# Gate, v and the ssm branch of a hybrid block in pairs of 512 columns: a quad of weights a step, 22 of 64 quads with seven block products, and memory pools opened part by part

## The chip, the cores and the metric

One core of a Trainium2 chip runs the whole program. Its engines run side by side, each its own list of instructions in order: TensorE (PE; its weight loads are shown apart as PEld), VectorE (DVE), ScalarE (ACT), GpSimd (POOL) and SyncE (SP), which here issues nearly all loads. Engines wait for each other and for DMAs through semaphores. The metric is the device time in microseconds (us) of one execution, the median of several runs. Line numbers such as L306 are lines of the kernel before; those of the changed kernel are named as such.

## The reference, cut to what matters

One layer of a hybrid block over 256 positions and 2048 channels, in f32: dilated window attention with 16 heads, beside a state space branch (SSD scan), both gated and merged.

```
hn = rms_norm(x, norm_w)
q, k, v, z_a, z_s, xbc, dt, g_a, g_s = split(hn @ w_in)
o_a = dilated_attention(q, k, v) * silu(z_a)
y = rms_norm(ssd_scan(silu(conv(xbc)), dt) * silu(z_s), ssm_norm_w)
merged = sigmoid(g_a) * (o_a @ w_attn_branch) + sigmoid(g_s) * (y @ w_ssm_branch)
out = rms_norm(x + merged @ w_out, final_norm_w)
```

Three of the products are touched: `hn @ v columns` (2048 by 2048), `y @ w_ssm_branch` (4096 by 2048) and `hn @ g_a columns` (2048 by 2048).

## The kernel before

**Products in f32 from two halves.** A weight tile w is rounded by ScalarE into a high part h (L201), and VectorE takes the low part l = w - h (L203). The left-hand side is split the same way. A block product is three matmuls into the same bank of PSUM: high by high, high by low, low by high.

**Weights.** The host lays all weights out in units of 128x1024 (512 KB), in the order in which they are used (`PLAN`); a unit is fetched, split and used once. They pass through one pool, `stream`, with four buffers each for w, h and l, which is open through the whole kernel. So SyncE may fetch four units ahead of TensorE at any place, across the end of a stage too. Rounding and low part are emitted at a raised priority (`L_AHEAD`), ahead of other work on their engines.

**Order of the stages.** Up to 590 us the ssm inputs xs and zs are projected, convolved and scanned, group by group, with the ssm gate gs. The scan writes y, split, into the tiles yT (L521: each by ScalarE L208 and VectorE L212). Then, with `gemm_b` (L283), one block of 512 columns at a time in two banks, one for each half of the rows:

- v (L572), 590 to 678 us: columns of `w_in`, left-hand side XT; ScalarE copies the banks into vt (L575).
- the ssm branch (L588), 678 to 854 us: left-hand side yT. Ahead of it four small matmuls (tot_y, L581) give the sum of squares of y, `rsqrt_rows` (L316) turns it into a factor by row, with one operation on GpSimd (L320), and two ScalarE operations apply it to the gate th_s (L587). Each finished bank is multiplied into th_s (L592).
- attention by heads (L635), 854 to 1160 us: q, k and za of each head, then scores, softmax and the mix with v, which stand some ticks behind (`after`, `tick`).
- the attention gate ga (L650), 1160 to 1250 us, into th_a.
- the attention branch (L671), from 1250 us, then the output product (L683) and the final norm.

`gemm_b` holds the inner loop, whose three matmuls are L306, L307 and L308:

```
for kt, i in steps:
    h, l = (a[:, kt % UB, :] for a in hl[kt // UB])
    pe.matmul(accs[i], xh, h, start=(kt == 0), stop=False)
    pe.matmul(accs[i], xh, l, start=False, stop=False)
    pe.matmul(accs[i], xl, h, start=False, stop=(kt == n_kt - 1))
```

The order of the instructions on each engine comes from a scheduler that simulates the program with its priorities. Constants (masks, distances, identity, ones) lie in one tile, cst, loaded once (L368).

Of the kernel before, what the change touches and what calls it, by code (L numbers as in the profile page):

```python
# [1 line left out]

# [1 line left out]

# [44 lines left out]
def weight_plan():  # L49
    plan = []  # L50

    def cols(tag, src, off, n_kt):
        plan.append((tag, "a", src, off, n_kt, P))

    def rows(tag, src, off, n_kt):
        plan.append((tag, "b", src, off, n_kt, 512))

    plan.append((("first", 0), "m", "w_in", (OFF_B, OFF_C, OFF_X, OFF_ZS), KT, 512))
    plan.append((("dt", 0), "a", "w_in", OFF_DT, KT, SH))
    for g in range(GROUPS):  # L60
# [9 lines left out]
    for c in range(4):  # L70
        rows(("v", c), "w_in", OFF_V + c * 512, KT)
    for c in range(4):
        rows(("ssm", c), "w_ssm_branch", c * 512, 2 * KT)
# [4 lines left out]
    for c in range(4):  # L78
        rows(("ga", c), "w_in", OFF_GA + c * 512, KT)
# [66 lines left out]


@with_exitstack
def hybrid_block(ctx: ExitStack, tc: tile.TileContext, wall, xt, x, pk_d, cst_d, fw_d, out):
# [19 lines left out]
    cst = cpool.tile([P, N_CST], F32, name="cst", tag="cst")  # L169
    dist_c, count_c = cst[:, 0:384], cst[:, 384:768]  # L170
    mask3 = cst[:, 768:1152]
    ident = cst[:, 1152:1280]
    ones = cst[:, 1280:1408]
    sel = cst[:, 1408:1536]
# [136 lines left out]
    def gates(tag, th, src, scales=(0.5, 0.5)):  # L311
        accs = gemm_b(tag, lambda kt: src[:, kt, :])
        for i in range(2):
            ac.activation(th[:, i, tag[1] * 512 : tag[1] * 512 + 512], accs[i], AF.Tanh, scale=scales[i])

    def rsqrt_rows(sums, n, name):  # L316
        var = lead.tile([P, 2], F32, name=f"var_{name}", tag="var", bufs=1)
        ve.tensor_scalar(var, sums, 1.0 / n, EPS, ALU.mult, ALU.add)
        r = lead.tile([P, 2], F32, name=f"r_{name}", tag="rr", bufs=1)
        gp.tensor_tensor(r, var, half, ALU.pow)  # L320
        hr = cpool.tile([P, 2], F32, name=f"hr_{name}", tag="hr", bufs=2)
        ve.tensor_scalar(hr, r, 0.5, None, ALU.mult)
        return r, hr

# [31 lines left out]
    def load_on(u):  # L356
        if u < 6:
            load(u + 4)
        if u < 3:
            nc.sync.dma_start(xr[:, 2 * u + 10 : 2 * u + 12, :], xt[:, 2 * u + 10 : 2 * u + 12, :])  # L360
        if u == 3:
            nc.sync.dma_start(pk[:, KT:], pk_d[:, KT:])
        if u == 6:

            for late in (th_s[:, 0, 0:1], cst[:, 0:1]):
                gp.tensor_copy(late, yT[0][:, 13, 0:1].bitcast(F32))
            nc.sync.dma_start(th_s, x.rearrange("(i p) d -> p i d", p=P))
# [19 lines left out]
    with tc.tile_pool(name="ssm", bufs=2) as sp:  # L387
        def dt_chain(acc):
            used = []

# [176 lines left out]
        gates(("gs", 3), th_s, XT)  # L567
        tick(final=True)

    with tc.tile_pool(name="att", bufs=2) as ap:  # L570
        vt = ap.tile([P, 2, D], F32, name="vt", tag="vt", bufs=1)
        for c in range(4):  # L572
            accs = gemm_b(("v", c), lambda kt: XT[:, kt, :])
            for i in range(2):
                ac.activation(vt[:, i, c * 512 : (c + 1) * 512], accs[i], AF.Copy)  # L575


        tot = bank("m1", 2, "tot_y")
        for i in range(2):
            for n in range(2):  # L580
                pe.matmul(  # L581
                    tot[:, 2 * i : 2 * i + 2], ssq[:, n, i * P : (i + 1) * P], ones[:, 0:2],
                    start=(n == 0), stop=(n == 1),
                )
        _, hr = rsqrt_rows(tot[:, 0:4:2], INNER, "y")
        for i in range(2):
            ac.activation(th_s[:, i], th_s[:, i], AF.Identity, scale=hr[:, i : i + 1], bias=hr[:, i : i + 1])  # L587
        for c in range(4):  # L588
            accs = gemm_b(("ssm", c), lambda kt: yT[kt // 16][:, kt % 16, :], n_kt=2 * KT)
            for i in range(2):  # L590
                g = th_s[:, i, c * 512 : (c + 1) * 512]
                ve.tensor_tensor(g, g, accs[i], ALU.mult)  # L592


        oaT = big.tile([P, 16, 2 * S], F32R, name="oaT", tag="yo0")

# [49 lines left out]
            evac(project(("za", h)), zh, f"za{h}", scale=0.5)  # L646
            half_silu(zh, za, f"za{h}")

        th_a = big.tile([P, 2, D], F32, name="th_a", tag="yo1")
        for c in range(4):  # L650
            gates(("ga", c), th_a, XT)
        tick(final=True)

    with tc.tile_pool(name="fin", bufs=2) as fp:
# [86 lines left out]
```

## Time and profile before

| what | before |
|---|---|
| median of 3 runs | 1421.44 us (1421.27 to 1422.06) |
| span of the profiled execution | 1419.2 us |
| TensorE busy | 1406.4 us (99%) |
| VectorE busy | 920.5 us (65%) |
| ScalarE busy | 760.2 us (54%) |
| bytes moved by DMA | 272.31 MB, mean 192 GB/s |

The span runs from the first to the last recorded instruction. The page gives no other time for the profiled execution, so the span stands beside the median. Shares of busy time are means over the whole span. Rows of groups give, behind the tiles, their shapes and a count: busy time in sum, mean ns of one instruction, and the engine's idle time just before them with what ended it. Rows of a timeline give the start, the duration and the instruction. Rows of windows give a stretch, the busy time and count on each engine, the clock granted to TensorE (1.00 is full), the DMAs' busy share and their rate.

### The profile page before, as it was taken

The page shows a single profiled execution, that of the slowest core. Times are in us where ns is not written, and L with a number is a line of the kernel's source. Part 1 is how long each engine was busy: PE and PEld are TensorE (multiplying, and loading weights), DVE is VectorE, ACT ScalarE, POOL GpSimd, SP SyncE. Part 2 cuts the span into 40 slices and gives each one's busy share as a digit, 9 for nine tenths or more (in the row PEclk, how much of TensorE's full clock was granted, in tenths as well). Part 3 has the DMA queues.
Part 4 walks back from the last instruction along what each step waited for, and adds up shares of the span by engine and source line. Part 5 has one row for each costly group of instructions (what it writes and reads, how often), then busy time and mean ns, then how long its engine had stood idle before and what let it go on. Part 6 is the DMA issues. An engine that isn't in the chain of part 4 may idle for free.

```text
span 1419.2 us, 19641 instructions
## 1 busy us (share of the span) xinstructions
PE 1406.4 (99%) x7404; PEld 1194.6 (84%) x7404; DVE 920.5 (65%) x1336; ACT 760.2 (54%) x1170; POOL 9.6 (1%) x63
## 2 busy tenths in 40 slices
PE   9999999999999999999999999999999999999997
PEld 7788888888888888888888888888888888888886
DVE  5978888877787888644444446666666654455654
ACT  6656766747575757444533334454544544444443
POOL 0000000000000000000000000000000000000000
PEclk9999999999999999999999999999999999999999
DMA  8566656566656665566566666555555557666663
GB/s 338 183 205 222 197 174 208 169 208 201 189 169 208 194 186 183 167 195 195 187 193 194 192 193 191 176 169 175 170 173 176 168 177 280 193 192 180 191 192 121
DMA packets 77759, 272.31 MB, mean 192 GB/s; under 512 B 8736, under 2 KB 9184, under 8 KB 77024
## 3 DMA queue, kind: packets, MB, share of 16 engines
q1 hardware_dynamic: 77088, 270.01, 60.5%
q8 instruction: 58, 0.95, 0.3%
q10 hardware_dynamic: 576, 1.05, 0.2%
q14 instruction: 37, 0.30, 0.1%
HBM read 268.86 MB, written 2.16 MB: 191 GB/s over the span
## 4 chain that ended last, share of the span: by engine, by line
PE 97%; DVE 1%; issue 0%; DMA 0%; ACT 0%; SPq 0%; POOL 0%; POOLq 0%; DVEq 0%; ACTq 0%
PE ps_xs L240 8%; PE ps_zs L240 8%; PE ps_xs L243 4%; PE ps_q L240 4%; PE ps_zs L243 4%; PE ps_za L240 4%; PE ps_k L240 4%; PE ps_ssm L306 4%; PE ps_ssm L308 4%; PE ps_ssm L307 4%; PE ps_za L243 2%; PE ps_k L243 2%; PE ps_q L243 2%; PE ps_v L306 2%; PE ps_attn L306 2%; PE ps_attn L308 2%
## 5 line engine op out<-in xcount | busy, mean ns | idle before, releaser
L203 DVE TENSOR_TENSOR l<-w,h 128x1024 fp32r<-128x1024 f32 (+1 forms) x481 | 583.1, 1215 | 430.6 <-ACT h L201 428.2
L201 ACT ACTIVATE h<-w 128x1024 fp32r<-128x1024 f32 (+1 forms) x481 | 505.3, 1052 | 573.2 <-PE ps_ssm L308 101.1
L240 PE MATMUL ps_xs<-XT,h 128*128 128x512 f32 x496 | 176.3, 397 | 0.0
L240 PE MATMUL ps_zs<-XT,h 128*128 128x512 f32 x496 | 175.8, 397 | 0.0
L243 PE MATMUL ps_xs<-XT,l 128*128 128x256 f32 x496 | 139.6, 281 | 0.0
L243 PE MATMUL ps_zs<-XT,l 128*128 128x256 f32 x496 | 139.0, 280 | 0.0
L240 PEld LDWEIGHTS ps_zs<-XT,h 128*128 128x128 f32 x496 | 93.1, 188 | 22.6
L240 PEld LDWEIGHTS ps_xs<-XT,h 128*128 128x128 f32 x496 | 93.2, 188 | 22.2
L308 PE MATMUL ps_ssm<-h,yT 128*128 128x512 f32 x256 | 99.6, 389 | 0.0
L307 PE MATMUL ps_ssm<-l,yT 128*128 128x512 f32 x256 | 99.6, 389 | 0.0
L306 PE MATMUL ps_ssm<-h,yT 128*128 128x512 f32 x256 | 99.4, 389 | 0.0
L243 PEld LDWEIGHTS ps_xs<-XT,l 128*128 128x128 f32 x496 | 93.6, 189 | 0.1
L243 PEld LDWEIGHTS ps_zs<-XT,l 128*128 128x128 f32 x496 | 93.6, 189 | 0.0
L240 PE MATMUL ps_q<-XT,h 128*128 128x512 f32 x256 | 90.4, 392 | 0.0
L240 PE MATMUL ps_za<-XT,h 128*128 128x512 f32 x256 | 89.6, 392 | 0.0
L240 PE MATMUL ps_k<-XT,h 128*128 128x512 f32 x256 | 89.6, 391 | 0.0
L243 PE MATMUL ps_q<-XT,l 128*128 128x256 f32 x256 | 74.5, 291 | 0.0
L243 PE MATMUL ps_k<-XT,l 128*128 128x256 f32 x256 | 71.7, 280 | 0.0
L243 PE MATMUL ps_za<-XT,l 128*128 128x256 f32 x256 | 71.7, 280 | 0.0
L240 PEld LDWEIGHTS ps_q<-XT,h 128*128 128x128 f32 x256 | 47.9, 187 | 10.6
L240 PEld LDWEIGHTS ps_k<-XT,h 128*128 128x128 f32 x256 | 47.9, 187 | 10.6
L240 PEld LDWEIGHTS ps_za<-XT,h 128*128 128x128 f32 x256 | 47.9, 187 | 10.6
(235 smaller groups left out, 2553.5 us busy)
## 6 DMA issues: line engine op xcount, KB each, us to landing
w<-in_wall SPq DMA_DIRECT2D x480, 512.0 KB, 3.6
acb<-acum_d SPq DMA_DIRECT2D x32, 256.0 KB, 3.2
th_s<-in_x SPq DMA_DIRECT2D x1, 2048.0 KB, 9.6
fin<-in_x SPq DMA_DIRECT2D x1, 2048.0 KB, 8.1
early<-in_xt SPq DMA_DIRECT2D x7, 256.0 KB, 7.0
fw<-in_fw SPq DMA_DIRECT2D x1, 1024.0 KB, 10.1
out<-fin SPq DMA_DIRECT2D x4, 256.0 KB, 2.9
out<-fin ACTq DMA_DIRECT2D x4, 256.0 KB, 3.2
```

Source lines behind the costliest of these rows:

```text
L201: ac.activation(h[:, a:b], w[:, a:b], AF.Copy)
L203: eng.tensor_tensor(l[:, a:b], w[:, a:b], h[:, a:b].bitcast(F32), ALU.subtract)
L240: pe.matmul(acc[:width], h[:, kk, :], m, start=(kt == 0), stop=False)
L243: pe.matmul(acc[:width, S:], l[:, kk, :], m[:, :S], start=False, stop=(kt == n_kt - 1))
L306: pe.matmul(accs[i], xh, h, start=(kt == 0), stop=False)
L307: pe.matmul(accs[i], xh, l, start=False, stop=False)
L308: pe.matmul(accs[i], xl, h, start=False, stop=(kt == n_kt - 1))
```

## The change

**Order.** The ssm branch now follows the scan at once, then the attention gate ga, then v, then attention by heads. v is written into one tile together with th_a (`yo1`).

**Quads.** The three products no longer use `gemm_b` but `quads`: two passes of 1024 columns. A step is a quad of weights, two blocks of 128 rows by two of 512 columns, laid out by the host for one load of 128x2048 (1 MB, `wq`, `lay_quads`). With two halves of the rows, a quad is a product of a 2x2 by a 2x2 matrix of blocks. All eight banks of PSUM are accumulators. Most quads take eight block products of three matmuls. 22 of the 64 (5 of 16 in each pass of the ssm branch, 3 of 8 in each of ga and v) take seven, in the manner of Strassen and Winograd: VectorE forms sums of the weight blocks (t13, t24), and sums of the left-hand blocks once for each product (`left`), all split into high and low parts; further sums on VectorE carry the products' accumulators into the four results. The ssm branch has three buffers for q and six for h and l each; ga and v have four and eight.

**Pools.** The weights' pools are opened by `stage` or for each part: one for the scan, `mid` for the ssm branch, `mid2` for ga and v, one for attention, one for the rest. A part's tiles lie where those of the part before lay. Of the constants, the distances and counts are loaded as masks when the attention part opens, and the identity a second time (ident2).

The diff, cut to its core:

```
+QPLAN = (("ssm", "w_ssm_branch", 0, 2 * KT), ("ga", "w_in", OFF_GA, KT), ("v", "w_in", OFF_V, KT))
...
-    stream = ctx.enter_context(tc.tile_pool(name="stream", bufs=4))
-    ev = ctx.enter_context(tc.tile_pool(name="ev", bufs=2))
...
+    @contextmanager
+    def stage(name):
+        nonlocal stream, ev
+        with (
+            tc.tile_pool(name=f"st_{name}", bufs=4) as stream,
+            tc.tile_pool(name=f"ev_{name}", bufs=2) as ev,
+            tc.tile_pool(name=name, bufs=2) as pool,
+        ):
+            yield pool
...
+    def left(tmp, src, n, h3, l3, h4, l4):
...
+            ve.tensor_tensor(x, v[:, js, :, :S].bitcast(F32), v[:, js, :, S:].bitcast(F32), ALU.add)
...
+            ve.tensor_tensor(s1, a22, a21, ALU.subtract)
+            ve.scalar_tensor_tensor(s2, s1, -1.0, a11, ALU.mult, ALU.subtract)
+            ve.tensor_tensor(s3, a11, a21, ALU.subtract)
+            ve.tensor_tensor(s4, a12, s2, ALU.add)
+            for r, h, l in ((raw[:, :, :3], h3[:, js], l3[:, js]), (s4, h4[:, js], l4[:, js])):
+                ac.activation(h, r, AF.Copy)
+                ve.tensor_tensor(l, r, h.bitcast(F32), ALU.subtract)
+
+    def quad(pool, deep, n, seven):
+        q = pool.tile([P, 2048], F32, name=f"q{n}", tag="q", bufs=deep[0])
+        nc.sync.dma_start(q, wq[n])
...
+            ac.activation(h[:, cut:], src[:, cut:], AF.Copy)
+            ve.tensor_tensor(l[:, cut:], src[:, cut:], h[:, cut:].bitcast(F32), ALU.subtract)
...
+        with tc.high_priority(L_AHEAD):
+            halves(q[:, :1024], ("12", "11"), 512 if seven else 0)
+            if seven:
...
+                ve.tensor_tensor(t24[:, :512], t13[:, :512], q[:, 1024:1536], ALU.add)
+                ve.tensor_tensor(t24[:, 512:], t24[:, :512], q[:, 1536:], ALU.add)
+            halves(q[:, 1024:], ("22", "21"))
+            if seven:
+                halves(t13, (5, 7))
+                halves(t24, (6, 4))
...
+            if u in lefts:
+                s1, s2, s3, s4 = lefts[u]
+                z = u == last
+                product(1, block(k0, 0), w["11"], z)
+                product(2, block(k1, 0), w["21"], end)
+                product(3, s4, w["22"], end)
+                product(7, s3, w[7], z)
+                product(5, s1, w[5], z)
+                product(6, s2, w[6], z)
+                product(4, block(k1, 1), w[4], end)
+            else:
+                for b, i, c in ((2, 0, "1"), (3, 0, "2"), (4, 1, "1"), (8, 1, "2")):
+                    product(b, block(k0, i), w["1" + c])
+                    product(b, block(k1, i), w["2" + c], end)
+            if u == last:
+                (p1, u4), (u3, u5) = sums
+                ac.activation(p1, accs[1], AF.Copy)
+                ve.tensor_tensor(u4, accs[6], p1, ALU.add)
+                ve.tensor_tensor(u3, accs[7], u4, ALU.add)
+                ve.tensor_tensor(u4, accs[5], u4, ALU.add)
+                ve.tensor_tensor(u5, accs[5], u3, ALU.add)
...
+    with tc.tile_pool(name="mid", bufs=2) as mid:
...
+        def gated(i, c, a, b, op):
+            g = th_s[:, i, c * 512 : (c + 1) * 512]
+            ve.tensor_tensor(b, a, b, op)
+            ve.tensor_tensor(g, g, b, ALU.mult)
...
+            quads(mid, (3, 6), "ssm", cc, lambda kt: yT[kt // 16][:, kt % 16, :], 2 * KT, order, lefts, sums, gated)
...
+    with tc.tile_pool(name="mid2", bufs=2) as mid:
...
+                quads(mid, (4, 8), tag, cc, lambda kt: XT[:, kt, :], KT, order, some, sums, finish)
+
+    with stage("att") as ap:
+        masks = ap.tile([P, 768], F32, name="masks", tag="masks", bufs=1)
+        nc.sync.dma_start(masks, cst_d[:, :768])
```

Three places in the built order follow. A row gives the line of its own kernel, the operation, the tile written and those read (numbers behind names tell copies of a tile apart), the shape, and in brackets the semaphores that the instruction waits for: an engine's name, or DMAHW for a DMA's landing.

SyncE at the end of the scan, where the next product's weights are fetched. Before, w193 and those behind it are the units of v:

```order
L187 DMA w191_6057<-in_wall 128x1024 [waits DMAHW2_49,DVE_49]
L187 DMA w192_6075<-in_wall 128x1024 [waits DMAHW3_49,DVE_49]
L187 DMA w193_6140<-in_wall 128x1024 [waits DMAHW4_49,DVE_49]
L187 DMA w194_6158<-in_wall 128x1024 [waits DMAHW5_49,DVE_49]
L187 DMA w195_6176<-in_wall 128x1024 [waits DMAHW6_49,DVE_49]
```

And in the changed kernel, where q0, q2, q4 and q1 are the first quads of the ssm branch:

```order
L205 DMA w191_6062<-in_wall 128x1024 [waits DMAHW3_49,DVE_49]
L205 DMA w192_6080<-in_wall 128x1024 [waits DMAHW4_49,DVE_49]
L615 DMA q0_6193<-in_wq 128x2048 [waits DMAHW5_49,DMAHW0_49,DMAHW6_49,DVE_49,DMAHW7_49,PE_49,Pool_49]
L615 DMA q2_6231<-in_wq 128x2048
L615 DMA q4_6265<-in_wq 128x2048
L615 DMA q1_6299<-in_wq 128x2048 [waits DMAHW1_49,DVE_49]
```

The first load behind the scan now waits for TensorE and GpSimd too, beside VectorE, and is one of three that leave together.

ScalarE at the same place, from the last square of y (xs15) on. Before, the copies that follow are those of v's weights:

```order
L514 ACTIVATE xs15_5739<-y1_15_6123 128x512 [waits DVE_49]
L208 ACTIVATE yT1_4244<-y1_15_6123,pk_75 128x256 x2
L201 ACTIVATE h197_6214<-w197_6212 128x1024 [waits DMAHW4_49,PE_49,Activation_49]
L201 ACTIVATE h198_6232<-w198_6230 128x1024 [waits DMAHW5_49,PE_49,Activation_49]
L201 ACTIVATE h199_6250<-w199_6248 128x1024 [waits DMAHW6_49,PE_49,Activation_49]
```

In the changed kernel the left-hand sums (sf_y, and a piece of yT0) and both scalings of th_s stand ahead of the first weights, h0_11:

```order
L538 ACTIVATE xs15_5744<-y1_15_6128 128x512 [waits DVE_49]
L226 ACTIVATE yT1_4249<-y1_15_6128,pk_69 128x256 x2
L610 ACTIVATE sf_y_6158<-tmp_6160 128x2x384 [waits PE_49,DVE_49,Activation_49,Pool_49]
L701 ACTIVATE th_s_103<-th_s_103,hr_y_6154 128x2048 [waits DVE_49]
L701 ACTIVATE th_s_103<-th_s_103,hr_y_6154 128x2048
L610 ACTIVATE yT0_92<-tmp_6160 128x2x128 [waits DVE_49]
L621 ACTIVATE h0_11_6195<-q0_6193 128x1024 [waits DMAHW1_49]
L621 ACTIVATE h0_21_6199<-q0_6193 128x1024
```

Four instructions came between the last piece of yT and the first copy of weights; the scalings (L701, before L587) came ahead of all of the branch's weights.

SyncE of the changed kernel where v ends and attention by heads begins (q62 and q63 are v's last quads, w193 holds the first weights of head 0):

```order
L615 DMA q62_8664<-in_wq 128x2048 [waits DMAHW3_49,DVE_49]
L615 DMA q63_8698<-in_wq 128x2048 [waits DMAHW4_49,DVE_49]
L753 DMA masks_8746<-in_cst 128x768 [waits DMAHW5_49,DMAHW6_49,DMAHW0_49,DMAHW7_49,DVE_49,PE_49]
L205 DMA w193_8754<-in_wall 128x1024
L205 DMA w194_8776<-in_wall 128x1024
L205 DMA w195_8802<-in_wall 128x1024
L205 DMA w196_8824<-in_wall 128x1024
L205 DMA w197_8854<-in_wall 128x1024 [waits DMAHW2_49,DVE_49]
```

The load of the masks, which waits for TensorE, now stands ahead of the first four units of attention; before, the units there followed each other with no such load between.

More of the change, by code (lines that the diff above doesn't have):

```diff
@@ L1 @@
-from contextlib import ExitStack, nullcontext
+from contextlib import ExitStack, contextmanager, nullcontext
 import numpy as np
@@ L168, in hybrid_block @@
     XT = big.tile([P, KT, 2 * S], F32R, name="XT", tag="xm")
[L169 to L174, printed above, removed]
+    ones2 = keep.tile([P, 2], F32, name="ones2", tag="ones2")
+    gp.memset(ones2, 1.0)
     nw, dsk = pk[:, 256:288], pk[:, 288:320]
@@ L331, in spread @@
         return rb
+    opened = ExitStack()
+    cpool = opened.enter_context(tc.tile_pool(name="const", bufs=1))
+    sp = opened.enter_context(stage("ssm"))
+    cst = cpool.tile([P, N_CST - 768], F32, name="cst", tag="cst")
+    mask3, ident = cst[:, 0:384], cst[:, 384:512]
+    ones, sel = cst[:, 512:640], cst[:, 640:768]
     early = big.tile([P, 28, S], F32, name="early", tag="yo1")
@@ L385, in hybrid_block @@
     acum_d = dram.tile([SH, S], F32, name="acum_d", tag="acum_d")
-    with tc.tile_pool(name="ssm", bufs=2) as sp:
+    with opened:
         def dt_chain(acc):
@@ new lines, in hybrid_block, with quads, product, block @@
+    BANKS = {1: "g", 2: "g", 6: "g", 3: "g", 7: "m1", 4: "m1", 5: "m2", 8: "m2"}
+    def quads(pool, deep, tag, cc, x_of, n_kt, order, lefts, sums, finish):
+        accs = {}
+        last = [u for u in order if u in lefts][-1]
+        def product(b, x, w, stop=False):
+            first = b not in accs
+            if first:
+                accs[b] = bank(BANKS[b], 4 if BANKS[b] == "g" else 2, f"ps_{tag}{cc}_{b}")
+            pe.matmul(accs[b], x[0], w[0], start=first, stop=False)
+            pe.matmul(accs[b], x[0], w[1], start=False, stop=False)
+            pe.matmul(accs[b], x[1], w[0], start=False, stop=stop)
+        def block(kt, i):
+            x = x_of(kt)
+            return x[:, i * P : (i + 1) * P], x[:, S + i * P : S + (i + 1) * P]
+        for n, u in enumerate(order):
+            w = quad(pool, deep, QFIRST[tag, cc] + u, u in lefts)
+            end = n == len(order) - 1
+            k0, k1 = 2 * u, 2 * u + 1
+            if u in lefts:
[19 more added lines that the diff above has]
+                ve.tensor_tensor(u5, accs[5], u3, ALU.add)
+        for i, c, b, op in (
+            (0, 0, 2, ALU.add), (0, 1, 3, ALU.subtract), (1, 0, 4, ALU.add), (1, 1, 8, ALU.subtract),
+        ):
+            finish(i, 2 * cc + c, accs[b], sums[i][c], op)
@@ L579, in hybrid_block @@
+    with tc.tile_pool(name="mid", bufs=2) as mid:
+        tot = bank("m2", 2, "tot_y")
         for i in range(2):
@@ new lines, in hybrid_block, with gate, value @@
+    yo1 = big.tile([P, 2, 2, D], F32, name="th_a", tag="yo1")
+    th_a, vt = yo1[:, 0], yo1[:, 1]
+    with tc.tile_pool(name="mid2", bufs=2) as mid:
+        sf = big.tile([P, 4, 2, 4, P], F32R, name="sf_x", tag="yo0")
+        h4, l4 = sf[:, :, 0], sf[:, :, 1]
+        left(
+            lambda: mid.tile([P, 1024], F32, name="tmp", tag="T", bufs=2), XT, 4,
+            h4[:, :, :3], l4[:, :, :3], h4[:, :, 3], l4[:, :, 3],
+        )
+        lefts = {2 * j + 1: [(h4[:, j, e], l4[:, j, e]) for e in range(4)] for j in range(4)}
+        def gate(i, c, a, b, op):
+            ve.tensor_tensor(b, a, b, op)
+            ac.activation(b, b, AF.Tanh, scale=0.5)
+        def value(i, c, a, b, op):
+            ve.tensor_tensor(b, a, b, op)
+        for tag, dst, finish in (("ga", th_a, gate), ("v", vt, value)):
+            for cc in range(2):
+                order = (0, 1, 2, 3, 4, 5, 6, 7) if cc or tag == "v" else (0, 2, 4, 1, 6, 3, 5, 7)
+                some = {u: lefts[u] for u in (1, 3, 5)}
+                sums = [[dst[:, i, (2 * cc + c) * 512 : (2 * cc + c + 1) * 512] for c in range(2)] for i in range(2)]
+                quads(mid, (4, 8), tag, cc, lambda kt: XT[:, kt, :], KT, order, some, sums, finish)
@@ L647, in hybrid_block @@
             half_silu(zh, za, f"za{h}")
-        th_a = big.tile([P, 2, D], F32, name="th_a", tag="yo1")
-        for c in range(4):
-            gates(("ga", c), th_a, XT)
         tick(final=True)
-    with tc.tile_pool(name="fin", bufs=2) as fp:
+    with stage("fin") as fp:
         fin = fp.tile([P, 2, D], F32, name="fin", tag="fin", bufs=1)
```

87 lines of the change are left out of this document (63 added, 24 removed).

## The prediction

> **What bounds the kernel now.** I read the page first (busy shares, then the chain that ended last), then the busy time stage by stage, then single stretches of the timeline.
>
> ```profile
> span 1419.2 us, 19641 instructions
> PE 1406.4 (99%) x7404; PEld 1194.6 (84%) x7404; DVE 920.5 (65%) x1336; ACT 760.2 (54%) x1170; POOL 9.6 (1%) x63
> PE 97%; DVE 1%; issue 0%; DMA 0%; ACT 0%; SPq 0%; POOL 0%; POOLq 0%; DVEq 0%; ACTq 0%
> ```
>
> TensorE is busy 99% of the span, and 97% of the chain is TensorE. An average can hide stages, so here are the three that the change rewrites: v, then the ssm branch, then the attention gate.
>
> ```profile
> core 0: us, PE busy (x) PEld busy (x) DVE busy (x) ACT busy (x) POOL busy (x), PEclk, DMA share, GB/s
> 590.00:678.00 88.00, 88.00 (x396) 72.74 (x392) 43.87 (x44) 39.45 (x45) 0.00 (x0) 1.00 0.61 187
> 678.00:854.00 176.00, 176.00 (x782) 145.92 (x782) 83.35 (x74) 73.22 (x68) 0.70 (x1) 1.00 0.62 192
> 1160.00:1250.00 90.00, 90.00 (x402) 74.61 (x401) 41.00 (x37) 39.97 (x44) 0.00 (x0) 1.00 0.67 223
> ```
>
> TensorE never rests there, and VectorE is busy only half of the time. So a matmul taken out shortens the span, VectorE has room, and any idle time put into TensorE's row lengthens the span by its full length.
>
> **What is removed.** 22 quads drop one of eight block products of three matmuls: 66 matmuls of 128x512.
>
> ```profile
> L306 PE MATMUL ps_ssm<-h,yT x256: 389/389/486, 678.5 to 852.1; 128*128 128x512 f32 x128
> ```
>
> One lasts 389 ns, but they overlap. The price is the spacing: 256 of this line and as many of L307 and L308 lie between the first start and the last, 765 steps in 173.6 us, or 0.227 us each. So 66 x 0.227 = **15.0 us** go. (66 x 0.389 = 25.7 us would be the mistake.)
>
> **What VectorE and ScalarE get.**
>
> ```profile
> L203 DVE TENSOR_TENSOR l<-w,h 128x1024 fp32r<-128x1024 f32 x473 | 577.9, 1224 | 428.8 <-ACT h L201 426.5
> L203 DVE TENSOR_TENSOR l<-w,h 128x512 fp32r<-128x512 f32 x8 | 5.3, 688 | 1.8 <-ACT h L201 1.7
> L592 DVE TENSOR_TENSOR th_s<-th_s,ps_ssm 128x512 f32<-128x512 f32 x8 | 5.1, 680 | 0.0
> L210 DVE TENSOR_TENSOR oaT<-za,oaT 128x256 fp32r<-128x256 f32 x16 | 6.7, 417 | 0.0
> L201 ACT ACTIVATE h<-w 128x1024 fp32r<-128x1024 f32 x473 | 500.6, 1059 | 571.7 <-PE ps_ssm L308 101.1 <-issue 68.1 <-PE ps_attn L308 50.7
> ```
>
> A quad of eight products costs VectorE 2 x 1.22 = 2.4 us beside 24 x 0.227 = 5.4 us of TensorE. A quad of seven costs 0.69 + 3 x 1.22 for the low parts and 1.22 + 2 x 0.69 for the weight sums, 7.0 us, beside 21 x 0.227 = 4.8 us. Alone it would hold TensorE up; mixed it need not. In the ssm branch: 10 x 7.0 + 22 x 2.4, some 16 us of accumulator sums and 11 us of left-hand sums, 151 us beside 738 x 0.227 = 167 us. In gate and v: 12 x 7.0 + 20 x 2.4 + 32 x 0.68 for the sums + 8.5 for the left-hand sums, 163 us beside 732 x 0.227 = 166 us. That is nearly level. The rings let VectorE run ahead by only 6 or 8 halves, so local stalls are likely. Below, nothing: the totals fit, and VectorE starts 6 us before TensorE there. Above, 12 quads x 2.2 us = 26 us, were nothing prepared ahead. I take **2 us**, near the lower end, since the totals fit. ScalarE has 1.06 us for each half and stays below both.
>
> **What the openings of the parts add.** The loads used to come from one ring through the whole kernel, so weights were fetched four units ahead across a stage's end. Now the first load of each part stands behind the release of the part before. Counted through the built order, the first load of the ssm branch waits for the last low part of yT, that of the gate for the last multiply into th_s, that of attention for the last v matmul, that of the last part for za's last matmul. TensorE has little or nothing to do meanwhile. Two prices first:
>
> ```profile
> w<-in_wall SPq DMA_DIRECT2D x480, 512.0 KB, 3.6
> fin<-in_x SPq DMA_DIRECT2D x1, 2048.0 KB, 8.1
> ```
>
> No load of 1024 KB stands in the trace; between these two rows, on a line, it lands after 5.1 us (bounds 3.6 and 8.1); 384 KB queued ahead add about 1.1 us.
>
> *Opening 1, ssm branch.* This is the place in the old trace:
>
> ```profile
> 587.81 2.82 PE L500 MATMUL yp<-gt,xdt 128*64 128x256 f32 x32
> 590.14 1.65 DVE L510 SCALAR_TENSOR_TENSOR y<-xs,pk,yp 128x256 f32<-128x256 f32 x4
> 590.56 0.50 PE L306 MATMUL ps_v<-h,XT 128*128 128x512 f32 x1
> 595.10 0.87 DVE L212 SCALAR_TENSOR_TENSOR yT<-y,pk,yT 128x256 fp32r<-128x256 f32 x2
> ```
>
> TensorE is free at 590.56 and today goes on with v. The last yT is written at 595.97. The load leaves then and lands at about 601.1. But ScalarE's order puts other work ahead of the first weights:
>
> ```profile
> 680.36 4.09 ACT L587 ACTIVATE th_s<-th_s,hr_y 128x2048 f32<-128x2048 f32 x2 [0.89 <-DVE hr_y L322]
> L320 POOL TENSOR_TENSOR r_y<-var_y,half 128x2 f32<-128x2 f32 x1 | 0.7, 700 | 125.1 <-DVE var_y L318 125.1
> ```
>
> After 595.97 VectorE does the first left-hand sum (1.22) and four pieces of about 0.42, with the row statistics among them (POOL 0.7): 598.7. ScalarE then does a 768-wide copy (0.84, between 0.62 for 512 and 1.06 for 1024), the two scalings of th_s (4.1 in all), which today hide behind weights that are ready, a 256-wide copy (0.41), and only then the first half of the first quad (1.06): 605.2. VectorE's low part comes so much later that TensorE loses 0.5 us more after four matmuls. Idle: 605.2 - 590.6 - 0.8 (tot_y) + 0.5 = **14.3 us**. If ScalarE's extra work were free, the load alone would give 602.2, 3 us less.
>
> *Opening 2, gate.* From the last matmul: its tail 0.16, two multiplies 1.36, a hop 0.1, the load 5.1, ScalarE 1.06, and 0.3 for the low part: **8.1 us** (6.6 to 11.1 by the load's bounds).
>
> *Opening 3, attention.* Tail and hop 0.26, the issue of masks 0.4 (issues take 0.33 to 0.46 us), w 3.6 with 1.1 for the masks ahead of it, ScalarE 1.06, VectorE 1.22 since the second matmul already needs the low part, less one matmul: **7.4 us** (5.9 without the masks' cost).
>
> *Opening 4, last part.* 0.26 + 3.6 + 1.06 + 1.22 less two matmuls (0.45) is 5.7 us. Here TensorE has the rest of attention to do:
>
> ```profile
> 904.89 0.59 PE L630 MATMUL ops<-pT,vt 128*128 128x256 f32 x2
> 905.54 0.49 PE L623 MATMUL ptp<-cst,p 128*128 128x128 f32 x3
> 906.34 0.47 PE L243 MATMUL ps_q<-XT,l 128*128 128x256 f32 x1
> ```
>
> One set of ops, ptp and sps takes 1.45 us, a second ops 0.65: 2.1 us are used, **3.6 us** idle.
>
> Together 33.4 us. Nothing at these ends is idle today, so nothing is given back.
>
> **The clock after a rest.**
>
> ```profile
> 1410.71 0.39 PE L308 MATMUL ps_out<-held,mT 128*128 128x512 f32 x1
> 1414.00:1415.00 1.00, 0.00 (x0) 0.00 (x0) 0.80 (x3) 0.24 (x1) 0.00 (x0) 1.00 0.13 45
> 1415.00:1416.00 1.00, 0.00 (x0) 0.00 (x0) 0.00 (x0) 0.00 (x0) 0.00 (x0) 0.52 1.03 383
> 1.34 4.38 PE L343 MATMUL warm<-ssq 128*128 128x256 f32 x10 [1.34 <-POOL raw_C L437]
> 5.38 1.28 PE L264 MATMUL ps_first<-yT,h 128*128 128x512 f32 x4
> ```
>
> After the last matmul (end 1411.1) the granted clock falls to half at about 1415, 3.9 us later. Openings 1 to 3 rest longer, so TensorE should come back at half speed. How long, the trace does not show at such a place; the nearest row is the start, where the warm-up matmuls fill the 4.0 us up to 5.38. At half speed for 4.0 us each loses 2.0 us: 6.0 us, less 0.8 us that are waits for low parts anyway: **5.2 us** (nothing to 8 us, the latter with opening 4).
>
> [...]
>
> **The rest.** At the start, 64 KB of ident are loaded ahead of some weights and the constants shrink from 768 to 384 KB: 0.2 us later, then 1.1 us earlier, beside loads that TensorE hardly waits for; I take nothing. fin and fw still load in the middle of the attention branch, with four units in hand.
>
> **The sum.** -15.0 + 2.0 + 33.4 + 5.2 = +25.6 us on the span of 1419.2: 1444.8. The median of the runs shown is 1421.44, 2.2 us above this span, which stays: **1447 us**.
>
> **The rivals.** *The clock is back at once*: -5.2, 1442 us. For it: the mean clock of 0.999 shows no loss today; against it: the fall above. 0.20. *VectorE becomes the bound in gate and v*: 163 against 166 us leaves nothing for hops. If each of its roughly 170 instructions there took 0.1 us more, it would need 180 us and TensorE would wait about 12 us more than I have: 1459 us. It decides once VectorE's sum passes TensorE's. 0.15. *Faster: the openings are covered.* A wait listed in the order could be for something long past, so that the first loads leave as early as today. Then the four rests vanish with their clock: -15.0 + 2.0, 1408 us. It decides where the four rests and the clock fall under 13 us in sum, about 3.2 us each. Against it: one load of 512 KB alone is 3.6 us, and the waits counted are for each part's last instructions. 0.05. *No change*: idle equal to the saving, 1421 us, from the same cause half present: 0.03. That the change does not remove 66 matmuls is excluded: the order of the built kernel holds 66 matmul instructions fewer than that of before.
>
> **How the numbers follow.** Forecast 0.57 at 1447 us. The clock rival lies 5 us below; with loads at their lower bounds as well that reaches 1437. VectorE's rival gives 1459; 1462 takes in most of it, with a loading time at its upper bound beside it. What is left out are the two faster cases and the rest of VectorE's, less than 2 in 10. Slower by over 0.2% (2.8 us, about what a measurement of this kernel can tell from no change): 0.92 (0.57 + 0.20 + 0.15); within: 0.03; faster: 0.05.
>
> **What would show it.** In the changed profile: TensorE idle of about 14, 8, 7 and 4 us at the four openings, ended by ScalarE's copy of the first weights, with SyncE's first load starting just after the last yT, the last multiply into th_s, and the last v matmul. In opening 1 the scalings of th_s must stand between. The granted clock must read 0.5 behind the first three. The stages' TensorE busy time must shrink by 15 us. Wrong would be loads that leave before the stage's end; or waits of TensorE for L622's low parts all through the gate and v.

## The result, and the profile after

The changed kernel takes 1458.78 us (median of 4 runs, 1458.27 to 1458.79), the kernel before 1421.68 us in the same runs: a ratio of 1.026, 95% interval 1.0245 to 1.0274. That is 37.1 us slower, inside the stated range, 11.8 us above the forecast.

The page of the profile after, its span, busy times and the chain that ended last:

```profile
span 1456.5 us, 19612 instructions
...
PE 1415.4 (97%) x7338; PEld 1190.1 (82%) x7338; DVE 1052.7 (72%) x1529; ACT 792.3 (54%) x1222; POOL 9.8 (1%) x64
...
PE 94%; DVE 3%; DMA 1%; issue 1%; ACT 1%; SPq 0%; POOL 0%; POOLq 0%; DVEq 0%; ACTq 0%
```

TensorE ran 66 matmuls fewer (7338, before 7404), and was busy 9 us **longer**. So idle time is not the whole loss: the matmuls themselves take longer somewhere. What TensorE waited for, as total, number of times and longest wait:

```profile
PE ps_ga L653 <- ACT h L621: 7.6, 1, 7.6
PE ps_ssm L653 <- issue: 7.5, 1, 7.5
PE ps_q L258 <- ACT h L219: 5.7, 1, 5.7
PE tot_y L695 <- DVE ssq L539: 3.9, 1, 3.9
PE ps_attn L324 <- ACT h L219: 2.1, 1, 2.1
...
PE ps_attn L325 <- DVE l L221: 0.5, 1, 0.5
PE ps_q L261 <- DVE l L221: 0.5, 1, 0.5
```

Waits that the kernel before has too, at the start and in gs (4.4 us in sum there, 5.0 us here), are left out. What remains are the four openings: 3.9 + 7.5 at the ssm branch, 7.6 at the gate, 5.7 + 0.5 at attention, 2.1 + 0.5 at the last part, 27.8 us in sum. No row names a low part in the quads (L622), so VectorE never held TensorE up inside them.

The same stages in windows (busy time and count by engine, granted clock, DMA share and rate):

```profile
605.00:612.00 7.00, 6.73 (x22) 5.43 (x23) 7.00 (x10) 5.94 (x8) 0.00 (x0) 0.73 0.50 178
612.00:700.00 88.00, 88.00 (x379) 70.85 (x378) 73.86 (x84) 44.91 (x49) 0.00 (x0) 1.00 0.55 194
...
787.00:793.00 6.00, 6.00 (x21) 4.77 (x21) 6.00 (x9) 5.51 (x7) 0.00 (x0) 0.78 1.00 423
793.00:873.50 80.50, 80.50 (x346) 64.76 (x345) 76.20 (x85) 45.71 (x53) 0.00 (x0) 1.00 0.64 231
...
965.00:972.00 7.00, 6.54 (x24) 5.24 (x24) 4.69 (x5) 4.06 (x4) 0.00 (x0) 0.60 0.85 312
...
1262.00:1268.00 6.00, 5.31 (x15) 3.92 (x16) 5.86 (x12) 4.61 (x8) 0.00 (x0) 0.72 0.89 312
```

Behind each opening the granted clock is low for some microseconds: 7.0 x 0.27 + 6.0 x 0.22 + 7.0 x 0.40 + 6.0 x 0.28 = some 7.7 us of full speed lost. Inside the stages the clock is 1.00, yet in the 88 us from 612 stand 379 matmuls, where before 396 stood in the 88 us of v. The matmuls of v, by operand (count, shortest, median and longest duration, first and last start), show it. First of the kernel after, then of before:

```profile
L653 PE MATMUL ps_v<-h,XT x98: 392/392/392, 873.5 to 958.2; 128*128 128x512 f32 x98
...
L655 PE MATMUL ps_v<-h,XT x98: 397/399/399, 874.0 to 958.7; 128*128 128x512 f32 x98
```

```profile
L306 PE MATMUL ps_v<-h,XT x128: 389/389/499, 590.6 to 677.0; 128*128 128x512 f32 x128
...
L308 PE MATMUL ps_v<-h,XT x128: 389/389/390, 591.1 to 677.5; 128*128 128x512 f32 x128
```

After: 366 matmuls, 365 steps in 85.2 us, 233.4 ns each. Before: 384, 383 steps in 86.9 us, 226.9 ns. With a full clock and no wait, each step takes 6.5 ns more. The code of the attention branch and the output is unchanged, and its matmuls are slower too; only the last 48, which stream from the tile held, keep their duration of 389 ns. What the two kernels don't share there is the **place of the weight tiles**. By the addresses in the built kernels, h and l start at a multiple of 256 bytes before, and at 128 (scan) or 96 (all later parts) bytes past one after the change, since the pool keep is opened ahead of them and holds a few small tiles.

### The profile page after: what moved, and what is told of

The parts are those of the page before. It is cut to its first block, busy times and chain, and to the rows that moved or that the text cites. A ratio compares the mean times of both kernels' runs of the same rounds, so it can differ in the third digit from the quotient of the medians.

```text
span 1456.5 us, 19612 instructions
## 1 busy us (share of the span) xinstructions
PE 1415.4 (97%) x7338; PEld 1190.1 (82%) x7338; DVE 1052.7 (72%) x1529; ACT 792.3 (54%) x1222; POOL 9.8 (1%) x64
## 4 chain that ended last, share of the span: by engine, by line
PE 94%; DVE 3%; DMA 1%; issue 1%; ACT 1%; SPq 0%; POOL 0%; POOLq 0%; DVEq 0%; ACTq 0%
PE ps_xs L258 8%; PE ps_zs L258 8%; PE ps_q L258 4%; PE ps_xs L261 4%; PE ps_zs L261 4%; PE ps_za L258 4%; PE ps_k L258 4%; PE ps_ssm L653 4%; PE ps_ssm L654 4%; PE ps_ssm L655 4%; PE ps_q L261 2%; PE ps_attn L325 2%; PE ps_attn L326 2%; PE ps_out L324 2%; PE ps_za L261 2%; PE ps_k L261 2%
## 5 line engine op out<-in xcount | busy, mean ns | idle before, releaser
L221 DVE TENSOR_TENSOR l<-w,h 128x1024 fp32r<-128x1024 f32 (+1 forms) x353 | 426.5, 1212 | 247.8 <-ACT h L219 244.2
L219 ACT ACTIVATE h<-w 128x1024 fp32r<-128x1024 f32 (+1 forms) x353 | 368.8, 1048 | 400.6 <-issue 62.9
L621 ACT ACTIVATE h<-q 128x1024 fp32r<-128x1024 f32 (+1 forms) x128 | 120.4, 980 | 91.6 <-PE ps_ssm L655 38.4
L622 DVE TENSOR_TENSOR l<-q,h 128x1024 fp32r<-128x1024 f32 (+1 forms) x128 | 140.0, 1128 | 21.5 <-ACT h L621 21.3
L653 PE MATMUL ps_ssm<-h,yT 128*128 128x512 f32 x216 | 79.7, 400 | 7.5 <-issue 7.5
L654 PE MATMUL ps_ssm<-l,yT 128*128 128x512 f32 x216 | 85.5, 399 | 0.0
L655 PE MATMUL ps_ssm<-h,yT 128*128 128x512 f32 x216 | 84.6, 395 | 0.0
L621 ACT ACTIVATE h<-t 128x1024 fp32r<-128x1024 f32 x44 | 45.7, 1056 | 50.2 <-PE ps_ssm L655 26.5
```

The costliest lines, as they stand in the source:

```text
L219: ac.activation(h[:, a:b], w[:, a:b], AF.Copy)
L221: eng.tensor_tensor(l[:, a:b], w[:, a:b], h[:, a:b].bitcast(F32), ALU.subtract)
L621: ac.activation(h[:, cut:], src[:, cut:], AF.Copy)
L622: ve.tensor_tensor(l[:, cut:], src[:, cut:], h[:, cut:].bitcast(F32), ALU.subtract)
L653: pe.matmul(accs[b], x[0], w[0], start=first, stop=False)
L654: pe.matmul(accs[b], x[0], w[1], start=False, stop=False)
```

## The experiments

**The place of the weight tiles: 32 bytes and 256 bytes.** Four kernels move tiles and do nothing else: pad32, pad512 and pad256 fill up the pools ahead of the weights in the changed kernel, before_shift32 moves the weight pool of the kernel before. The first diff is that of pad32; the fillings are 104 and 56 elements in pad512, 40 and 56 in pad256. The second is that of before_shift32.

```
+    keep.tile([P, 8], F32, name="fill2", tag="fill2")
...
+    cpool.tile([P, 8], F32, name="fill3", tag="fill3")
```

```
+    shift = ctx.enter_context(tc.tile_pool(name="shift", bufs=1))
+    shift.tile([P, 8], F32, name="fill2", tag="fill2")
     stream = ctx.enter_context(tc.tile_pool(name="stream", bufs=4))
```

> The changed kernel with 32 bytes of filling in each of the pools keep and const, so that every weight tile h and l lies at a multiple of 64 bytes again, as it did before the change; nothing else is altered. Theory: the 128x512 matmuls that stream h and l from places 32 bytes past such a multiple are spaced 233.3 ns instead of 227.0 ns. 738 + 732 + 384 + 336 = 2190 of them at 6.3 ns are 13.8 us: 1445.0 us, and the spacing in the ssm branch falls to 227 ns. Rival: the spacing comes from eight open banks or from a busier VectorE: no change, 1458.8 us and 233 ns.

> The kernel before, with its weight pool moved by 32 bytes and nothing else. Theory of the place of the tiles: v, ssm branch, gate, attention branch and output hold 384 + 768 + 384 + 384 + 336 = 2256 matmuls that stream h or l; at 6.3 ns more each 14.2 us: 1435.9 us, and the last 48 matmuls, which stream from held, stay at 227 ns. Rival (the spacing comes from what the quads do): no change, 1421.7 us.

> The changed kernel, filled up so that all pools behind keep start at a multiple of 512 bytes, as the weight pool did before the change; nothing else is altered. A multiple of 64 (pad32) did not bring the 227 ns back: its h and l lay at 128 past a multiple of 256, and those of before at a multiple of 512. Theory that the place of h and l decides, at 256 or 512 bytes: spacing 227 ns in ssm branch, gate, v, attention branch and output, 2190 x 6.3 ns = 13.8 us less than 1458.8: 1445.0 us. Rival, the place of other tiles or the work beside it decides: 232 to 233 ns as in pad32, 1459 to 1462 us.

> The same filling, but to 256 past a multiple of 512 bytes for every weight tile h and l. If a multiple of 256 is enough: 1445.0 us and 227 ns, as pad512. If it must be 512: 232 to 233 ns and 1459 to 1462 us. If pad512 does not help either, both stay at 1459 to 1462 us.

Measured, with the bytes by which h and l stand past a multiple of 256, and the spacing in v from the rows below, worked out as above:

| kernel | past 256 | spacing in v, ns | us | ratio to before (95% interval) |
|---|---|---|---|---|
| before | 0 | 226.9 | 1421.68 | 1 |
| before_shift32 | 32 | 233.7 | 1440.51 | 1.0136 (1.0119 to 1.0153) |
| after | 96, scan 128 | 233.4 | 1458.78 | 1.0260 (1.0245 to 1.0274) |
| pad32 | 128, scan 192 | 232.3 | 1462.11 | 1.0288 (1.0273 to 1.0303) |
| pad512 | 0 | 226.8 | 1443.06 | 1.0153 (1.0135 to 1.0171) |
| pad256 | 0 | 226.6 | 1442.85 | 1.0150 (1.0134 to 1.0166) |

The rows for v of before_shift32, pad32, pad512 and pad256, a first and a last line of each:

```profile
L308 PE MATMUL ps_v<-h,XT x128: 393/396/499, 591.4 to 680.4; 128*128 128x512 f32 x128
...
L310 PE MATMUL ps_v<-h,XT x128: 393/394/397, 592.0 to 680.9; 128*128 128x512 f32 x128
```

```profile
L655 PE MATMUL ps_v<-h,XT x98: 390/393/405, 875.1 to 959.5; 128*128 128x512 f32 x98
...
L657 PE MATMUL ps_v<-h,XT x98: 390/393/405, 875.6 to 959.9; 128*128 128x512 f32 x98
```

```profile
L655 PE MATMUL ps_v<-h,XT x98: 389/389/389, 865.2 to 947.5; 128*128 128x512 f32 x98
...
L657 PE MATMUL ps_v<-h,XT x98: 388/389/389, 865.7 to 948.0; 128*128 128x512 f32 x98
```

```profile
L655 PE MATMUL ps_v<-h,XT x98: 389/389/389, 865.6 to 947.9; 128*128 128x512 f32 x98
...
L657 PE MATMUL ps_v<-h,XT x98: 388/389/389, 866.0 to 948.3; 128*128 128x512 f32 x98
```

The first expectation named the wrong number: a multiple of 64 bytes (pad32) does not bring the spacing back, and the kernel is 3.3 us slower still. The traces put this mostly in attention by heads: from the first matmul of q to the last of za it takes 296.2 us there, and 292.4 us in the changed kernel. A multiple of 256 does (226.6 ns in pad256), and 512 adds nothing (226.8 ns in pad512). before_shift32 shows the effect without any quad, in the kernel before: 19.2 us over the 1421.33 us of before beside it, more than the 14.2 us expected. The sum left out gs and the weights of attention, which are moved too: from q to za it now takes 293.5 us, where it took 289.6. pad256 gives the price in the changed kernel: 1458.78 - 1442.85 = **15.9 us**. It fits the count: 738 + 732 + 384 + 336 matmuls at 233.4 - 226.9 = 6.5 ns are 14.2 us, and the 384 matmuls of gs in the scan, spaced 4.8 ns more than before (below), add 1.8 us.

**Is it the place of every tile, or of those that TensorE streams?** before_pad moves, in the kernel before, the tiles of the scan and of attention from 96 and 160 to 0 and 64 bytes past a multiple of 256, and leaves the weights.

```
     crT = cpool.tile([P, SH], F32, name="crT", tag="crT")
+    cpool.tile([P, 40], F32, name="fill2", tag="fill2")
```

> The kernel before, with 160 bytes of filling in the constants, so that the tiles of the scan and of attention (bt to y, qT, fin) start at a multiple of 256 or of 64 bytes; the weight ring and XT stay where they are. Theory that only the place of the tiles that TensorE itself streams counts: no change, 1421.4 us, and the matmuls of gs stay at the 234 ns that they have beside the scan. Rival, the places of the tiles that VectorE and ScalarE work on count as well: gs falls to the 229.6 ns of pad256, 384 x 4.6 ns = 1.8 us, and with what the heads gain some 2 to 4 us: 1418 to 1419.6 us.

Measured: 1420.50 us, ratio 0.9991 (0.9982 to 1.0001), no change that can be told; in v the spacing is the same as before. The expectation also misread a number: matmuls of gs that follow one another without a wait (start to start under 300 ns) are spaced 227.5 ns in the kernel before, not 234, and 232.3 ns in the changed one; they stay at 227.4 here. So the place of the weights counts, and the place of the scan's and attention's own tiles does not, as far as these runs can tell. Streaming is not all of it, though. In q, k and za TensorE streams XT, which lies in the same place in all kernels, and h and l are the other operand, whose loading the profile shows as PEld. Still two matmuls of k that follow one another start 175.4 ns apart in the mean in the kernel before, 178.1 ns in before_shift32 and 177.2 ns in pad32, but 175.2 ns in the changed kernel. No run separates this smaller effect from the other tiles moved with the weights.

**The waits at the openings.** tilewaits lets each pool wait tile by tile for what lay in its place.

```
-            tc.tile_pool(name=f"st_{name}", bufs=4) as stream,
-            tc.tile_pool(name=f"ev_{name}", bufs=2) as ev,
-            tc.tile_pool(name=name, bufs=2) as pool,
+            tc.tile_pool(name=f"st_{name}", bufs=4, reuse_waits="tile") as stream,
+            tc.tile_pool(name=f"ev_{name}", bufs=2, reuse_waits="tile") as ev,
+            tc.tile_pool(name=name, bufs=2, reuse_waits="tile") as pool,
...
-    with tc.tile_pool(name="mid", bufs=2) as mid:
+    with tc.tile_pool(name="mid", bufs=2, reuse_waits="tile") as mid:
...
-    with tc.tile_pool(name="mid2", bufs=2) as mid:
+    with tc.tile_pool(name="mid2", bufs=2, reuse_waits="tile") as mid:
```

> The changed kernel, where the pools of the parts wait tile by tile for what lay in their place, not for the whole pool before (one option of each pool). The loads of all four openings then leave before the stage ahead has ended. Theory that the instruction orders of ScalarE and VectorE bind openings 1 and 2 as they stand: opening 1 unchanged (first weights still behind the scalings of th_s, 605.3 us), opening 2 shorter by 1.4 us, opening 3 by 5 us and 2.8 us of half clock, opening 4 by 1 to 3 us: about 1447 us. Rival, the loads alone bind each opening: openings 2 to 4 vanish with their half clock and opening 1 shrinks by some 3 us: 1434 us. Second rival, the waits are inferred wrongly: 1458.8 us.

Measured: 1447.23 us (1.0187, 1.0172 to 1.0202), 11.6 us less than the changed kernel. Its waits of TensorE:

```profile
PE ps_ssm L653 <- ACT h L621: 8.1, 1, 8.1
PE ps_ga L653 <- ACT h L621: 5.9, 1, 5.9
PE tot_y L695 <- DVE ssq L539: 3.9, 1, 3.9
...
PE ps_q L261 <- DVE l L221: 1.3, 1, 1.3
```

Openings 1 and 2 are still there (2 is 1.7 us shorter), opening 3 is down from 6.2 us to 1.3 us and opening 4 from 2.6 us to 1.3 us. Why opening 1 stays is seen on SyncE and ScalarE: the loads now leave at 589.05, where they left at 596.73 in the changed kernel, and ScalarE's first copy of a weight still starts at 603.91 (604.13). First SyncE and ScalarE of tilewaits (start, duration, instruction), then of the changed kernel:

```profile
589.05 1.28 SPq L615 DMA_DIRECT2D q<-in_wq  x3
```

```profile
598.88 0.84 ACT L610 ACTIVATE sf_y<-tmp 128x768 fp32r<-128x768 f32 x1 [3.08 <-DVE hr_y L340]
599.63 4.07 ACT L701 ACTIVATE th_s<-th_s,hr_y 128x2048 f32<-128x2048 f32 x2
603.60 0.40 ACT L610 ACTIVATE yT<-tmp 128x256 fp32r<-128x256 f32 x1
603.91 3.88 ACT L621 ACTIVATE h<-q 128x1024 fp32r<-128x1024 f32 x4
```

```profile
596.73 1.28 SPq L615 DMA_DIRECT2D q<-in_wq  x3
```

```profile
599.10 0.84 ACT L610 ACTIVATE sf_y<-tmp 128x768 fp32r<-128x768 f32 x1 [3.23 <-DVE hr_y L340]
599.85 4.06 ACT L701 ACTIVATE th_s<-th_s,hr_y 128x2048 f32<-128x2048 f32 x2
```

ScalarE's list, not the transfer, ends opening 1; the load was a second wait hidden behind it. The rival in which the loads alone bind falls.

**The order at the openings.** early adds to tilewaits what its expectation names; its core:

```
+        pre = {u: quad(mid, (3, 6), QFIRST["ssm", 0] + u, False) for u in (0, 2, 4)}
+        dep = one_after(pre[4])
...
-            ac.activation(th_s[:, i], th_s[:, i], AF.Identity, scale=hr[:, i : i + 1], bias=hr[:, i : i + 1])
...
+            ac.activation(b, b, AF.Copy, scale=hr[:, i : i + 1])
+            ve.scalar_tensor_tensor(g, g, 1.0, b, ALU.add, ALU.mult)
```

> tilewaits, and beside it the orders of ScalarE and VectorE at the openings: the first three quads of the ssm branch and of the gate are written ahead of the left-hand sums, the left-hand sums are made to wait for the third of these quads (by a factor of one made from its weights), the scalings of th_s are taken out and the factor is applied to the sums of each pass instead, and the load of the masks stands behind the first loads of attention. Theory (the orders bound openings 1 and 2 of tilewaits): the ssm branch starts at about 597 us instead of 605, and with its low parts at 599; the gate's first low part comes at 782.5 us by the clock of the changed kernel instead of 788.6; about 8.3 + 1.6 (half clock) + 5 + 1.3 = 16 us less than 1447.2: 1431 us. Rival, VectorE cannot give the left-hand sums in time behind the first quads, and TensorE waits at the first quads with seven for what was saved: 1440 us or more.

Measured: 1449.08 us (1.0197, 1.0179 to 1.0215), no faster than tilewaits. The ssm branch does start earlier, at 598.7 us instead of 605.0, but stops at its first quad with seven products. TensorE's row there:

```profile
622.37 0.73 PE L663 MATMUL ps_ssm<-h,sf_y 128*128 128x512 f32 x2 [0.89 <-ACT h L631]
623.73 0.50 PE L664 MATMUL ps_ssm<-l,sf_y 128*128 128x512 f32 x1 [0.62 <-DVE l L632]
625.50 0.50 PE L663 MATMUL ps_ssm<-h,sf_y 128*128 128x512 f32 x1 [0.58 <-ACT h L631]
```

24 matmuls from there on take 3.4 us more than their neighbours, and at the same place in the gate 3.2 us more. The rival has the time right, and that TensorE stops at these quads. But what TensorE waits for, by these rows, are the halves of the weights: VectorE is at the left-hand sums until 621.8 us and forms this quad's last sum of weights only at 623.6 us. These 6.6 us are only a part of the 18 us by which the theory missed. By the lists of waits TensorE waits 6.3 us less in early than in tilewaits (14.2 and 20.5 us, waits of the start and gs left out), yet it is busy 3.2 us longer (1418.7 and 1415.5 us). The kernel's weight tiles lie at 160 bytes past a multiple of 256 (192 in the scan), with a spacing of 234.2 ns in v, so some of this may be their place; that was not separated.

**The price of the quads with seven.** eight takes eight products in every quad.

```
-        last = [u for u in order if u in lefts][-1]
+        last = ([None] + [u for u in order if u in lefts])[-1]
...
-        lefts = {2 * j + 1: [(h4[:, j, e], l4[:, j, e]) for e in range(4)] for j in range(4)}
+        lefts = {}
```

> The changed kernel with eight block products in all 64 quads; left-hand sums, weight sums and accumulator sums are left out. Theory that TensorE bounds the quads: 66 matmuls more at 233 ns are 15.4 us, less some 1.7 us because no left-hand sums stand ahead of the first weights at openings 1 and 2: 1472.5 us. Rival, VectorE bounds the quads with seven: what they save is given back in stalls, 1459 us or less.

Measured: 1473.04 us (1.0362, 1.0346 to 1.0377), 14.3 us more than the changed kernel, though its openings are 2.8 us shorter by its list of waits, since no left-hand sums stand there. No wait inside the quads is listed in either kernel. So the 22 quads do save what their matmuls cost and give nothing back inside the quads; a part of it they give back at the openings.

**One ring for all.** onering opens the weight pool once, ahead of everything, and the quads draw from it; the order of the quads is that of the changed kernel. onering_late moves the first quads with seven back in the first passes of the ssm branch and the gate (the diff shows the former), and onering_18 adds to it that gate and v take two of them a pass instead of three.

```
+    stream = ctx.enter_context(tc.tile_pool(name="stream", bufs=4))
...
-        q = pool.tile([P, 2048], F32, name=f"q{n}", tag="q", bufs=deep[0])
-        nc.sync.dma_start(q, wq[n])
+        qa, qb = (stream.tile([P, UNIT], F32, name=f"q{n}_{e}", tag="w", bufs=W_BUFS) for e in range(2))
+        nc.sync.dma_start(qa, wq[n, :, :UNIT])
+        nc.sync.dma_start(qb, wq[n, :, UNIT:])
...
-            ((0, 2, 4, 1, 6, 8, 3, 10, 12, 5, 11, 9, 13, 7, 14, 15), (1, 0, 2, 3, 4, 6, 5, 8, 10, 7, 11, 12, 9, 13, 14, 15))
+            ((0, 2, 4, 6, 8, 1, 10, 3, 12, 5, 11, 9, 13, 7, 14, 15), (1, 0, 2, 3, 4, 6, 5, 8, 10, 7, 11, 12, 9, 13, 14, 15))
...
-                some = {u: lefts[u] for u in (1, 3, 5)}
+                some = {u: lefts[u] for u in (1, 5)}
```

> The quads and the order of the changed kernel, with the weight pool opened once for the whole kernel as before the change (a quad is two loads of 512 KB into the ring of four w, four h and four l; only the halves of the weight sums have rings of three or four of their own), at a multiple of 512 bytes; the masks load behind the first weights of attention. Theory (openings, their half clock and the place of the tiles are all that outweighs the 66 matmuls): the idle time of the four openings, 27.8 us, and about 6 us of half clock go from the 1443.1 us of pad512: 1409 us, which is 12 to 13 us under the kernel before, as the 15.0 us of the saved matmuls say less a few stalls. Rival: rings of four let VectorE run ahead too little, and each quad with seven costs TensorE a wait of its own: 22 times up to 1 us, 1420 to 1430 us.

> onering, with the first quad with seven two places later in the first pass of the ssm branch and one place later in that of the gate. Theory that the left-hand sums, which VectorE can only begin once y is finished, are late for the first such quad (early lost 3.4 us there, and 3.2 us in the gate): 2 to 6 us less than onering. Rival, they are in time in onering, since TensorE no longer rests and VectorE has the first quads' low parts ready ahead: the same within 1 us.

> onering_late, with two quads of seven products a pass instead of three in gate and v (18 of 64 instead of 22): 12 matmuls more. Theory that VectorE bounds gate and v there, as the waits for low parts and for accumulator sums in these stages say (5.6 us more than in pad256): the waits of 5 to 6 us go, 12 x 0.227 = 2.7 us come: 1414 us. Rival, the waits come from the shallow ring and stay: 1420 us.

Measured: onering 1421.28 us (0.9998, 0.9988 to 1.0007), onering_late 1417.01 us (0.9968, 0.9957 to 0.9979), onering_18 1413.13 us (0.9935, 0.9922 to 0.9947). All openings are gone; TensorE of onering_18 goes from the scan into the ssm branch without a gap:

```profile
587.83 2.82 PE L527 MATMUL yp<-gt,xdt 128*64 128x256 f32 x32
590.58 0.50 PE L655 MATMUL ps_ssm<-h,yT 128*128 128x512 f32 x1
```

But 1409 us was not reached: in onering TensorE waits two times 1.2 us at the first quads with seven of the ssm branch, and 6.1 us in sum in the gate and v (the rival with its 1420 to 1430 us held). The later first quads with seven were worth 4.3 us. What then was left in onering_late is in the gate and v, where TensorE waits 4.1 us for low parts and sums of VectorE and 1.3 us for copies of ScalarE; these are its windows, and behind them those of onering_18:

```profile
759.00:846.00 87.00, 85.00 (x368) 67.89 (x367) 81.27 (x102) 48.27 (x55) 0.00 (x0) 1.00 0.58 189
846.00:934.00 88.00, 84.64 (x367) 67.95 (x366) 72.59 (x85) 43.97 (x50) 0.00 (x0) 1.00 0.62 198
```

```profile
759.00:843.00 84.00, 84.00 (x372) 69.55 (x371) 73.98 (x92) 46.09 (x53) 0.00 (x0) 1.00 0.60 193
843.00:929.00 86.00, 85.34 (x376) 70.28 (x375) 63.74 (x71) 40.77 (x45) 0.00 (x0) 1.00 0.65 206
```

VectorE is busy 81.3 of 87 us in the gate. With four quads of seven fewer in gate and v it is busy 74.0 of 84, TensorE's waits in both are down to 0.7 us, and although 12 matmuls came back the kernel is 3.9 us faster. onering_18 beats the kernel before by 8.4 us.

## Why the prediction was right, and where it was short

**Where the time landed.** The direction and the mechanism of the openings were forecast, and the runs show them. That 1458.78 us still lies inside the range is luck: its upper end was drawn for VectorE's rival and for slow loads, neither of which came, and a cost that the prediction did not have filled the place.

**Matmuls removed, -15.0 us.** Right: 66 of them, and eight, which has them back, is 14.3 us slower. But the sign that was named, 15 us less busy time of TensorE, did not show: it was busy 9 us longer, as each matmul took longer. The stretch shown for the gate, 1160 to 1250 us, was also misplaced: its matmuls start from 1143.9 to 1232.7 us. TensorE does not rest there either, so nothing hangs on it.

**VectorE's stalls in the quads, 2 us.** There were none in the changed kernel, where the rings hold six or eight halves. With rings of four (onering) there were. VectorE's sum was also reckoned too large: it was busy 152.7 us from 779 to 959 us, around gate and v, and not 163 us. The rival in which VectorE bounds gate and v gave 1459 us, the measured time to the microsecond, and was still **wrong**: its sign, a wait of TensorE for L622, is missing in the profile. A time alone does not tell a mechanism.

**The openings, 33.4 us.** Right in place and cause, too large in sum: 27.8 us of idle time (11.4, 7.6, 6.2 and 2.6 us where 14.3, 8.1, 7.4 and 3.6 were forecast). At opening 1 the scan ended 1.4 us later on TensorE, while y was finished only 0.6 us later (596.6), so that less of the chain stood alone. The 1 MB load, taken as 5.1 us, landed after 5.0 us in the median of all 64; the trace of before does hold one load of 1024 KB, that of fw, which landed after 10.1 us. That ScalarE's scalings of th_s, not the load, end opening 1 was shown by tilewaits.

**The clock after a rest, 5.2 us.** Right in kind, larger: 7.7 us by the windows. After openings 1 and 2 the matmuls have their full-clock duration again (0.39 us, where they took 0.63 us at a clock of 0.50) 3.5 and 3.1 us after the restart, after opening 3 only after 5.9 us, of which the first 1.3 us are one matmul and a wait for its low part; from its first unbroken matmul on (966.0 us) it is 4.6 us. The 4.0 us that the prediction took for each of the three was an estimate from the row of the start. Opening 4 counts as well.

**The step that failed** is the price of a matmul: the prediction took the 0.227 us of the kernel before as that of all matmuls to come, and under "The rest" took nothing for moved tiles. The spacing is not a constant of the instruction: it was 233 ns here, for 2190 matmuls in five products, and 232 ns for gs. pad256 prices this at 15.9 us. Set against the terms: -15.0 + 27.8 + 7.7 + 15.9 = 36.4 us beside 37.1 measured. Against pad256, which is the change without this term, the forecast of 1447 us is 4 us too high: the openings were too large by 5.6 us and the stalls by 2.0, the clock too small by 2.5, which leaves about 1 us open.

**The other rivals.** The clock was not back at once. The openings were not covered, and 66 matmuls did go.

## What to carry to other kernels

When a change opens or reorders memory pools, look at the start addresses of the tiles that TensorE streams, before and after: here a few small tiles ahead of them cost 15.9 us, more than the 14.3 us by which eight shows the saving, and filling tiles gave it back (pad256). A pool that is opened anew at a stage's end was an emptied pipeline here: its first load, the first copies in each engine's list and a low clock came one behind the other, 27.8 us of idle time and 7.7 us of clock in sum, and taking one of them away showed the next (tilewaits, 11.6 us less). Count a saving on TensorE in the stage in which the other engines' lists can still keep up; here 18 quads with seven products were 3.9 us faster than 22.

## What the runs showed of the hardware that was not expected

In v, the 128x512 matmuls in f32 were spaced 226.6 to 226.9 ns where the tile they stream starts at a multiple of 256 bytes (before, pad512, pad256), and 233.7, 233.4 and 232.3 ns where it starts 32, 96 and 128 bytes past one (before_shift32, the changed kernel, pad32); in before and the changed kernel the granted clock in v is 1.00. Other places were not timed alone (early, at 160, has 234.2 ns).

The clock fell after a rest shorter than the 3.9 us seen at the end of the kernel before. At opening 4 the longest single wait was 2.1 us, with one of 0.5 us soon after it; for 2 us from the first matmul on the granted clock was still 1.00, then 0.51. Windows of TensorE of the changed kernel there:

```profile
1260.00:1262.00 2.00, 0.10 (x1) 0.00 (x0) 0.93 (x5) 0.94 (x1) 0.00 (x0) 1.00 0.92 369
1262.00:1264.00 2.00, 1.31 (x5) 0.79 (x6) 1.86 (x5) 2.00 (x5) 0.00 (x0) 1.00 1.00 403
1264.00:1267.00 3.00, 3.00 (x9) 2.32 (x8) 3.00 (x8) 2.17 (x3) 0.00 (x0) 0.51 0.83 262
```

The length of the wait alone does not decide it. In tilewaits the waits at this place are only 0.3 and 1.0 us, and the clock still falls, as the durations of 0.63 us show:

```profile
1253.84 0.72 PE L324 MATMUL ps_attn<-h,oaT 128*128 128x512 f32 x2 [0.33 <-ACT h L219]
1255.52 0.64 PE L325 MATMUL ps_attn<-l,oaT 128*128 128x512 f32 x1 [0.97 <-DVE l L221]
1255.95 0.63 PE L326 MATMUL ps_attn<-h,oaT 128*128 128x512 f32 x1
```

In early the waits there are 0.3 and 1.0 us, and no matmul of this product lasts longer than 0.50 us. In the changed kernel's trace the granted clock is half from 595.07 to 608.72, 782.80 to 789.63, 963.71 to 970.54 and 1264.08 to 1267.50 us, for 13.65, 6.83, 6.83 and 3.41 us at the four openings: 4, 2, 2 and 1 times 3.41 us. What decides when it falls and comes back, no run here shows.

So here a rest was paid 2 us after it, in a stretch that looks busy (3.00 of 3.00 us at a clock of 0.51); whoever searches for it reads the column of the granted clock, not that of the busy time.
